# Mixers without GpSimd, latents with tokens on the partitions, and an output projection of plain fp32 products

## The chip, the core and the metric

The kernel runs on one core of a Trainium2 chip. The metric is the time of one execution on the device, in microseconds: the median of several runs. Of the core's engines the text speaks of TensorE (PE; PEld is its weight load), VectorE (DVE), ScalarE (ACT), GpSimd (POOL) and SyncE (SP), whose queue issues the weight loads.

## What is computed

The reference is a trunk of two layers over 256 tokens of width 1024 in fp32. One layer is

```python
x = x + 0.5 * swiglu(rms_norm(x, norm_ffn1[l]), ffn1_w13[l], ffn1_w2[l])
h = rms_norm(x, norm_mix[l])
proj = h @ w_in[l]
z, xbc, dt_raw, cq, ckv, kidx, widx, xl, gl = jnp.split(proj, offsets, axis=-1)
...
mixed = jnp.concatenate([y_ssd, y_att, y_lru], axis=-1)
x = x + mixed @ w_out[l]
x = x + 0.5 * swiglu(rms_norm(x, norm_ffn2[l]), ffn2_w13[l], ffn2_w2[l])
```

Between the two lines of `proj` and `mixed` stand three causal mixers. `ssd_mixer` (512 columns of `mixed`) passes `xbc` through a convolution of width 4 and a silu, forms a decay-weighted product over the tokens, multiplies by silu(z) and normalizes two groups of 256 columns per token: `rms_norm(yg, norm_g)`. `dsa_mixer` (256 columns) normalizes the latents `cq`, `ckv` and the index key `kidx` per token, selects 64 keys per query by an index score, and attends to them. `rglru_mixer` (256 columns) is a convolution, a linear recurrence over the tokens and a gate gelu(gl).

## The kernel before

Products of weights and activations are made of three fp32r products: each operand is split into a rounded part and a rest. `wsplit` does that for weights: ScalarE rounds (`whi`, L249), and another engine subtracts (`wlo`, L250). In the FFNs (`ffn`, L305) that other engine is DVE; in `mixers` (L367) the argument `eng` says which: DVE for the latents and the LRU input, GpSimd (G) for `xbc`, the gate `gl`, `z` and all of `w_out`. `mm3` (L239) and `mmt` (L253) issue the three products.

The mixers first project the latents (L399 to L416): `pair` and `block` put 128 columns of w_in on the partitions of PSUM and the 256 tokens along the row. The norms' sums of squares come from TensorE products with a column of ones (L423, L426), and the small columns are transposed back to tokens (L451). Then come the index score and the selection (`scores`, `select`), softmax and attention (`logits`, `softmax`, `weigh`), the decay matrices M0 and M1 (L643 on), the LRU (`lru`), four `xbc_pair`s with the convolution (`conv`, L668) and the silu, the gate (`lru_gate`), `z`, and the SSD products (L778, L779). At the end the group norm's factor is computed per token (L788 to L796), spread over the partitions by four transposes (L800), multiplied into y (L806), y is split (L808, L809), and `project` (L817) multiplies by w_out: first the LRU rows, then the attention rows, then the SSD rows, into four PSUM accumulators that stay open over all three. The last step adds them to the residual `X` (L832) and calls `finish`, which begins the next norm (`norm_block`, L272).

The program's order is not the source's: a scheduler places the instructions of every engine by its own simulated times, and each engine then runs its list in order. Weights come through a pool of four buffers (`wraw`) that the loads in SP's queue use in turn; the split parts have four buffers each. PSUM is in three pools: `gu` (three buffers), `acc` (two) and `sm` (three).

## Time and profile before

| | |
|---|---|
| median of 3 runs | 1076.36 us (1075.48 to 1077.21) |
| profiled execution | 1075.42 us, its span 1073.7 us |
| TensorE, DVE, ScalarE, GpSimd busy | 994.8, 699.1, 530.8, 139.9 us |
| mean granted clock of TensorE | 0.971 |
| read from HBM | 170.57 MB, 160 GB/s over the span |

The profile is one execution on the chip. Busy times are sums over the whole span and mix two kinds of stage, the FFNs and the mixers; a stretch has to be cut out to see what limits it. Matmuls are pipelined, so the duration of one is longer than the distance to the next one's start. Layer 0's mixers lie between about 211 and 358 us, layer 1's between about 734 and 881 us.

### The profile page before, as it was taken

How to read it: one execution, taken by the hardware profiler on the slowest of the kernel's cores; microseconds unless marked ns; L12 is line 12 of the kernel's file. 1: busy time of each engine (PE TensorE's matmuls, PEld its weight loads, DVE VectorE, ACT ScalarE, POOL GpSimd, SP SyncE). 2: the span in 40 equal slices, each digit the busy share in tenths (PEclk: the TensorE clock that was granted, in tenths of full speed). 3: DMA queues.
4: the chain of work that ended last, by engine and by line, in shares of the span. 5: the costliest groups of instructions: out<-in, count | busy, mean ns of one | idle time of the engine just before them, and what ended most of it. 6: DMA issues, size and time to landing. Idle time of an engine off the chain costs nothing.

```text
span 1073.7 us, 13352 instructions
## 1 busy us (share of the span) xinstructions
PE 994.8 (93%) x5003; PEld 832.7 (78%) x5003; DVE 699.1 (65%) x1221; ACT 530.8 (49%) x814; POOL 139.9 (13%) x91
## 2 busy tenths in 40 slices
PE   3999999999577999999999999999986779999998
PEld 2888888889475788888888888889876658888886
DVE  3666664579995766564566656455999666665643
ACT  4444544458442655454555544455765345454432
POOL 5100000034463000000000000002364310000000
PEclk9999999999788999999999999999997889999999
DMA  8855555553143366555656655566320435565560
GB/s 184 260 182 180 172 181 196 179 156 99 40 139 116 115 200 191 166 178 181 216 165 196 195 174 182 179 202 186 99 79 27 150 118 175 180 193 162 191 215 20
DMA packets 144833, 172.48 MB, mean 161 GB/s; under 512 B 4899, under 2 KB 116657, under 8 KB 144769
## 3 DMA queue, kind: packets, MB, share of 16 engines
q1 hardware_dynamic: 143840, 171.03, 49.8%
q0 software_dynamic: 896, 0.60, 1.0%
q8 instruction: 39, 0.64, 0.2%
q14 instruction: 26, 0.21, 0.1%
q10 hardware_dynamic: 32, 0.01, 0.0%
HBM read 170.57 MB, written 1.05 MB: 160 GB/s over the span
## 4 chain that ended last, share of the span: by engine, by line
PE 78%; DVE 18%; DMA 2%; ACT 1%; issue 1%; SPq 0%; ACTq 0%; DVEq 0%
PE gu L255 16%; PE gu L256 16%; PE gu L257 15%; PE acc L255 8%; PE acc L256 8%; PE acc L257 8%; DVE xbc L668 4%; PE sm L339 2%; DMA wraw<-in_ffn_w_dram 2%; DVE score L523 1%; DVE score L535 1%; DVE m L746 1%; DVE wlo L250 1%; PE gu L241 1%; DVE m L532 1%; PE gu L240 1%
## 5 line engine op out<-in xcount | busy, mean ns | idle before, releaser
L250 DVE TENSOR_TENSOR wlo<-wraw,whi 128x1024 fp32r<-128x1024 f32 x274 | 335.0, 1224 | 264.9 <-ACT whi L249 256.1
L249 ACT ACTIVATE whi<-wraw 128x1024 fp32r<-128x1024 f32 x322 | 337.7, 1052 | 314.0 <-PE gu L257 155.7
L255 PE MATMUL gu<-whi,xh 128*128 128x512 f32 x704 | 278.0, 398 | 11.3 <-ACT whi L249 9.6
L257 PE MATMUL gu<-whi,xl 128*128 128x512 f32 x704 | 276.6, 396 | 0.2
L256 PE MATMUL gu<-wlo,xh 128*128 128x512 f32 x704 | 274.7, 392 | 0.0
L250 POOL TENSOR_TENSOR wlo<-wraw,whi 128x1024 fp32r<-128x1024 f32 (+2 forms) x48 | 111.5, 2335 | 706.1 <-ACT whi L249 704.0
L255 PEld LDWEIGHTS gu<-whi,xh 128*128 128x128 f32 x704 | 132.9, 189 | 37.2 <-ACT whi L249 10.0
L257 PEld LDWEIGHTS gu<-whi,xl 128*128 128x128 f32 x704 | 132.6, 188 | 27.8 <-DVE xl L282 1.0
L256 PEld LDWEIGHTS gu<-wlo,xh 128*128 128x128 f32 x704 | 132.9, 189 | 27.3 <-DVE wlo L250 0.8
L257 PE MATMUL acc<-whi,hl 128*128 128x512 f32 x352 | 137.7, 391 | 0.0
L256 PE MATMUL acc<-wlo,hh 128*128 128x512 f32 x352 | 137.1, 389 | 0.0
L255 PE MATMUL acc<-whi,hh 128*128 128x512 f32 x352 | 135.7, 391 | 0.0
L240 PE MATMUL gu<-xh,whi 128*128 128x256 f32 (+1 forms) x320 | 94.4, 299 | 27.5 <-DVE cx L681 26.6
L241 PE MATMUL gu<-xl,whi 128*128 128x256 f32 (+1 forms) x320 | 95.1, 298 | 0.0
L242 PE MATMUL gu<-xh,wlo 128*128 128x256 f32 (+1 forms) x320 | 92.8, 291 | 0.0
L240 PEld LDWEIGHTS gu<-xh,whi 128*128 128x128 f32 (+1 forms) x320 | 61.8, 195 | 30.1 <-ACT th L674 26.9
L257 PEld LDWEIGHTS acc<-whi,hl 128*128 128x128 f32 x352 | 66.1, 188 | 13.6
L256 PEld LDWEIGHTS acc<-wlo,hh 128*128 128x128 f32 x352 | 66.1, 188 | 13.6
L255 PEld LDWEIGHTS acc<-whi,hh 128*128 128x128 f32 x352 | 66.1, 188 | 13.3
L334 ACT ACTIVATE th_s<-gu,rhalf 128x256 f32<-128x256 f32 x88 | 41.8, 475 | 69.0 <-PE gu L257 68.8
L241 PEld LDWEIGHTS gu<-xl,whi 128*128 128x128 f32 (+1 forms) x320 | 62.4, 195 | 2.2 <-issue 1.4
L242 PEld LDWEIGHTS gu<-xh,wlo 128*128 128x128 f32 (+1 forms) x320 | 62.4, 195 | 0.1
(350 smaller groups left out, 962.8 us busy)
## 6 DMA issues: line engine op xcount, KB each, us to landing
wraw<-in_ffn_w_dram SPq DMA_DIRECT2D x184, 512.0 KB, 4.8
wraw<-in_ffn_w_dram SPq DMA_DIRECT2D x40, 1024.0 KB, 5.0
...
wraw<-in_w_out_dram SPq DMA_DIRECT2D x8, 512.0 KB, 3.6
...
```

The source lines that it names most:

```text
L240: T.matmul(o, lh, rh, start=first, stop=False)
L241: T.matmul(o, lh, rl, start=False, stop=False)
L242: T.matmul(o, ll, rh, start=False, stop=last)
L249: S.activation(hi[sl], raw, AF.Copy)
L250: eng.tensor_sub(lo[sl], raw, hi[sl].bitcast(F32))
L255: T.matmul(o, xh, wh, start=first, stop=False)
L256: T.matmul(o, xh, wl, start=False, stop=False)
L257: T.matmul(o, xl, wh, start=False, stop=last)
L334: S.activation(th, ps[h][:, 0:256], AF.Tanh, scale=rh_[:, h:h + 1])
L339: T.transpose(pt[:, j * SEQ + h * P:j * SEQ + (h + 1) * P], hf[:, j * P:(j + 1) * P], ident)
L523: V.scalar_tensor_tensor(s2, rel[:, p_, :ns], wx[:, qb, hd:hd + 1], score, ALU.mult, ALU.add)
L668: V.scalar_tensor_tensor(dst[:, j, s:], xr[:, j, :SEQ - s], col(wname, l, (3 - s) * wm + m), dst[:, j, s:], ALU.mult, ALU.add)
```

## The change

- GpSimd has no more work in the mixers: all splits of w_in and the product of M0 go to DVE.
- The latents (460 columns, dt and the index key and weights among them) are projected with the tokens on the partitions, as in the FFN: three products of up to 460 columns for each of 8 rows of blocks and 2 halves of the tokens. ScalarE evicts them with the norm's factor per token as scale and sums their squares by rows; cq and ckv are transposed after that. The index key's rsqrt joins that of the other two.
- The output projection takes y, the attention and LRU outputs, and w_out as plain fp32, one product each, with no split. The attention and LRU rows are added to the residual first; the SSD rows are scaled by `ssd_norm` on ScalarE, and the group norm's factor is applied per token where the two halves of the groups are evicted into the residual: eight evictions in place of four.

```diff
-        ah, al = two("ah", 1, F32R), two("al", 1, F32R)
-        rh, rl = two("rh", 1, F32R), two("rl", 1, F32R)
+        ya_, yl_ = two("ya_", 1), two("yl_", 1)
...
-        raw0 = load_cols(C_DT, 264)
-        raw1 = load_cols(C_CKV, 196)
-        pcq = pair(raw0, 8, (V, V))
...
+        NS = C_XL - C_DT
+        O = 32 - (C_CQ - C_DT)
+        pS = [psg.tile([P, 512], F32, name="gu")[:, :NS] for _ in range(NH)]
+        for q in range(2):
+            raw = rp.tile([P, 4, 512], F32, name="wraw")
+            nc.sync.dma_start(raw[:, :, :NS], w_in[q * 512:(q + 1) * 512, C_DT:C_XL]
+                              .rearrange("(k p) c -> p k c", p=P))
+            ws = [wsplit([P, 2, 512], [((slice(None), slice(None), slice(0, NS)), raw[:, 2 * i:2 * i + 2, :NS])], V)
+                  for i in range(2)]
+            for h in range(NH):
+                hs = slice(h * P, (h + 1) * P)
+                for k in range(4):
+                    kk = 4 * q + k
+                    mmt(pS[h], n.h[kk][:, hs], n.l[kk][:, hs], ws[k // 2][0][:, k % 2, :NS],
+                        ws[k // 2][1][:, k % 2, :NS], kk == 0, kk == KD - 1)
+        cs = mp.tile([P, NH, 512], F32, name="cs", bufs=1)
+        for h in range(NH):
+            S.activation(cs[:, h, O:O + NS], pS[h], AF.Copy, scale=n.r[:, h:h + 1])
+        o_q, o_kv, o_ki, o_wi = (O + c - C_DT for c in (C_CQ, C_CKV, C_KI, C_WI))
+        lss = mp.tile([P, 3, NH], F32, name="lss", bufs=1)
+        for h in range(NH):
+            for i, (o, w) in enumerate(((o_q, 256), (o_kv, 128), (o_ki, 64))):
+                sq = mp.tile([P, 256], F32, name="lsq", bufs=1)
+                S.activation(sq[:, :w], cs[:, h, o:o + w], AF.Square, accum_out=lss[:, i, h:h + 1])
+        cq, ck = two("cq", 1), one("ck", 1)
+        ptq = att_ps()
+        ptk = att_ps()
         for h in range(NH):
             hs = slice(h * P, (h + 1) * P)
             for b in range(2):
-                T.matmul(pss[:, h:h + 1], sqc[:, b, hs], ones[:, 0:1], start=b == 0, stop=b == 1)
-        for h in range(NH):
-            hs = slice(h * P, (h + 1) * P)
-            T.matmul(pss[:, 2 + h:3 + h], sqc[:, 2, hs], ones[:, 0:1], start=True, stop=True)
-        r2 = mp.tile([P, NH], F32, name="r2", bufs=1)
-        V.tensor_mul(r2, n.r, n.r)
-        vc = mp.tile([P, 2, NH], F32, name="vc", bufs=1)
-        for i, dim in enumerate((256, 128)):
-            V.scalar_tensor_tensor(vc[:, i], pss[:, 2 * i:2 * i + 2], 1.0 / dim, r2, ALU.mult, ALU.mult)
-        V.tensor_scalar(vc, vc, RS, EPS * RS, ALU.mult, ALU.add)
-        sc = mp.tile([P, 2, NH], F32, name="sc", bufs=1)
+                T.transpose(ptq[:, b * SEQ + h * P:b * SEQ + (h + 1) * P], cs[:, h, o_q + b * P:o_q + (b + 1) * P], ident)
+            T.transpose(ptk[:, hs], cs[:, h, o_kv:o_kv + P], ident)
+        for b in range(2):
+            V.tensor_scalar(cq[:, b], ptq[:, b * SEQ:(b + 1) * SEQ], col("cq_norm", l, b), None, ALU.mult)
+        V.tensor_scalar(ck, ptk[:, :SEQ], col("ckv_norm", l, 0), None, ALU.mult)
+        vc = mp.tile([P, 3, NH], F32, name="vc", bufs=1)
+        for i, dim in enumerate((256, 128, 64)):
+            V.tensor_scalar(vc[:, i], lss[:, i], RS / dim, EPS * RS, ALU.mult, ALU.add)
+        sc = mp.tile([P, 3, NH], F32, name="sc", bufs=1)
         rsqrt_of(sc, vc, mp, "cr")
-        V.tensor_mul(sc, sc, n.r[:, None, :].to_broadcast([P, 2, NH]))
 
...
-        kss = mp.tile([P, NH], F32, name="kss", bufs=1)
-        ksq = mp.tile([P, NH, 64], F32, name="excl0", bufs=1)
-        S.activation(ksq, sm[:, :, 0:64], AF.Square)
-        V.tensor_reduce(kss, ksq, axis=AX.X, op=ALU.add)
-        kr = mp.tile([P, NH], F32, name="kr", bufs=1)
-        rsqrt(kr, kss, 1.0 / 64, mp, "kq")
         for h in range(NH):
-            V.scalar_tensor_tensor(TI[:, h, 4:6], sm[:, h, None, 0:64].to_broadcast([P, 2, 64]), kr[:, h:h + 1],
-                                   kig[:, l, None, :].to_broadcast([P, 2, 64]), ALU.mult, ALU.mult)
+            V.scalar_tensor_tensor(TI[:, h, 4:6], cs[:, h, None, o_ki:o_ki + 64].to_broadcast([P, 2, 64]),
+                                   sc[:, 2, h:h + 1], kig[:, l, None, :].to_broadcast([P, 2, 64]),
+                                   ALU.mult, ALU.mult)
...
-            S.copy(ah[:, :, qs], pt2)
-            V.tensor_sub(al[:, :, qs], pt2, ah[:, :, qs].bitcast(F32))
+            S.copy(ya_[:, :, qs], pt2)
...
-            ps = pair(load_cols(C_GL, 256), 0, (G, G))
+            ps = pair(load_cols(C_GL, 256), 0, (V, V))
...
-                V.scalar_tensor_tensor(gt[:, b], gt[:, b], 1.0, hx[:, b], ALU.add, ALU.mult)
-                S.copy(rh[:, b], gt[:, b])
-                V.tensor_sub(rl[:, b], gt[:, b], rh[:, b].bitcast(F32))
+                V.scalar_tensor_tensor(yl_[:, b], gt[:, b], 1.0, hx[:, b], ALU.add, ALU.mult)
...
-        xbc_pair(load_cols(C_XBC + 512, 256), 4, (G, G), picked)
-        xbc_pair(load_cols(C_XBC + 768, 256), 6, (G, G), picked)
+        xbc_pair(load_cols(C_XBC + 512, 256), 4, (V, V), picked)
+        xbc_pair(load_cols(C_XBC + 768, 256), 6, (V, V), picked)
...
-            G.tensor_mul(M0[g], M0[g], cb[:, None, :SEQ].to_broadcast([P, 4, SEQ]))
+            V.tensor_mul(M0[g], M0[g], cb[:, None, :SEQ].to_broadcast([P, 4, SEQ]))
             V.tensor_mul(M1[g], M1[g], cb[:, None, SEQ:].to_broadcast([P, 4, P]))
 
-        xbc_pair(load_cols(C_XBC, 256), 0, (G, G))
-        xbc_pair(load_cols(C_XBC + 256, 256), 2, (G, G))
+        xbc_pair(load_cols(C_XBC, 256), 0, (V, V))
+        xbc_pair(load_cols(C_XBC + 256, 256), 2, (V, V))
...
-            ps = pair(load_cols(C_Z + 256 * q, 256), 0, (G, G))
+            ps = pair(load_cols(C_Z + 256 * q, 256), 0, (V, V))
...
 
 
-        pss = small_ps()
+
+        w_out = A["w_out"][l]
+
+        def rows_of(k0, c):
+            raw = rp.tile([P, 4, 512], F32, name="wraw")
+            nc.sync.dma_start(raw, w_out[k0 * P:(k0 + 4) * P, c * 512:(c + 1) * 512]
+                              .rearrange("(k p) c -> p k c", p=P))
+            return raw
+
+        def project(ys, ws, h, c, scale=None):
+            acc = psg.tile([P, 512], F32, name="gu")
+            for t, (y, w) in enumerate(zip(ys, ws)):
+                T.matmul(acc, y[:, h * P:(h + 1) * P], w, start=t == 0, stop=t == len(ys) - 1)
+            xs = X[h][:, c * 512:(c + 1) * 512]
+            if scale is None:
+                V.tensor_add(xs, acc, xs)
+            else:
+                V.scalar_tensor_tensor(xs, acc, scale, xs, ALU.mult, ALU.add)
+
+        rest = [ya_[:, 0], ya_[:, 1], yl_[:, 0], yl_[:, 1]]
+        for c in range(2):
+            raw = rows_of(4, c)
+            for h in range(NH):
+                project(rest, [raw[:, t] for t in range(4)], h, c)
+
+        raws = [rows_of(0, c) for c in range(2)]
+        for c in range(2):
+            for t in range(4):
+                S.activation(raws[c][:, t], raws[c][:, t], AF.Copy, scale=col("ssd_norm", l, t))
+        yr = []
         for q in range(2):
+            pss = small_ps()
             sq = two("z", 2)
             S.activation(sq, yg[q], AF.Square)
             V.tensor_add(sq[:, 0], sq[:, 0], sq[:, 1])
             for h in range(NH):
-                T.matmul(pss[:, 2 * q + h:2 * q + h + 1], sq[:, 0, h * P:(h + 1) * P], ones[:, 0:1],
-                         start=True, stop=True)
-        yr = mp.tile([P, 2, NH], F32, name="yr", bufs=1)
-        yv = mp.tile([P, 4], F32, name="yv", bufs=1)
-        V.tensor_scalar(yv, pss[:, :4], RS / 256, 4.0 * EPS * RS, ALU.mult, ALU.add)
-        rsqrt_of(yr.rearrange("p q h -> p (q h)"), yv, mp, "yq")
-        pb = small_ps().rearrange("p (q t) -> p q t", q=2)
+                T.matmul(pss[:, h:h + 1], sq[:, 0, h * P:(h + 1) * P], ones[:, 0:1], start=True, stop=True)
+            yv = mp.tile([P, NH], F32, name="yv", bufs=2)
+            V.tensor_scalar(yv, pss[:, :NH], RS / 256, 4.0 * EPS * RS, ALU.mult, ALU.add)
+            r = mp.tile([P, NH], F32, name="yr", bufs=2)
+            rsqrt_of(r, yv, mp, "yq")
+            yr.append(r)
         for q in range(2):
             for h in range(NH):
-                bcast_rows(pb[:, q, h * P:(h + 1) * P], yr[:, q, h:h + 1])
-        sh = []
-        for q in range(2):
-            t = mp.tile([P, 2, 2, SEQ], F32R, name="m0", bufs=2)
-            for j in range(2):
-                b = 2 * q + j
-                V.scalar_tensor_tensor(yg[q][:, j], yg[q][:, j], col("ssd_norm", l, b), pb[:, q, :],
-                                       ALU.mult, ALU.mult)
-                S.copy(t[:, 0, j], yg[q][:, j])
-                V.tensor_sub(t[:, 1, j], yg[q][:, j], t[:, 0, j].bitcast(F32))
-                sh.append((t[:, 0, j], t[:, 1, j]))
-
-
-        accs = [[psa.tile([P, 512], F32, name="acc") for _ in range(NH)],
-                [psg.tile([P, 512], F32, name="gu") for _ in range(NH)]]
-        w_out = A["w_out"][l]
-
-        def project(k0, parts, eng, step):
-
-            nk = len(parts)
-            for c in range(2):
-                raw = rp.tile([P, nk, 512], F32, name="wraw")
-                nc.sync.dma_start(raw, w_out[k0 * P:(k0 + nk) * P, c * 512:(c + 1) * 512]
-                                  .rearrange("(k p) c -> p k c", p=P))
-                ws = [wsplit([P, 2, 512], [(slice(None), raw[:, i:i + 2])], eng) for i in range(0, nk, 2)]
-                for h in range(NH):
-                    hs = slice(h * P, (h + 1) * P)
-                    for t, (xh, xl) in enumerate(parts):
-                        mmt(accs[c][h], xh[:, hs], xl[:, hs], ws[t // 2][0][:, t % 2], ws[t // 2][1][:, t % 2],
-                            step == 0 and t == 0, step == 2 and t == nk - 1)
-                    if step == 2:
-                        xs = X[h][:, c * 512:(c + 1) * 512]
-                        V.tensor_add(xs, accs[c][h], xs)
+                for c in range(2):
+                    project([yg[q][:, 0], yg[q][:, 1]], [raws[c][:, 2 * q], raws[c][:, 2 * q + 1]], h, c,
+                            yr[q][:, h:h + 1])
+                    if q == 1:
                         finish(h, c)
-
-        project(6, [(rh[:, b], rl[:, b]) for b in range(2)], G, 0)
-        project(4, [(ah[:, b], al[:, b]) for b in range(2)], G, 1)
-        project(0, sh, G, 2)
 
 
     n = norm_begin()
```

How the scheduler orders it is read from the built programs, layer 0; "x2" is two rows alike.

DVE, from the convolution of the first two xbc pairs on (L668 before and L657 now are the convolution step, L250 the subtraction of a split, L585, L586 and L575, L576 softmax). Before:

```order
L668 SCALAR_TENSOR_TENSOR xbc<-cx,colT_104,xbc 128x255 x4
L713 SCALAR_TENSOR_TENSOR lb<-lt,lb 128x512
L668 SCALAR_TENSOR_TENSOR xbc<-cx,colT_104,xbc 128x254
L585 SCALAR_TENSOR_TENSOR prob<-ya,prob 128x1024
L668 SCALAR_TENSOR_TENSOR xbc<-cx,colT_104,xbc 128x254 x3
L715 SCALAR_TENSOR_TENSOR la_2413<-la,lb 128x256 x2
```

and now:

```order
L250 TENSOR_TENSOR wlo<-wraw,whi 128x1024
L710 TENSOR_TENSOR lx<-gu,nrb 128x512
L578 SCALAR_TENSOR_TENSOR mx<-mx,qr 128x4
L525 MATCH_REPLACE score_2056<-m_2051,score_2048 128x128
L700 SCALAR_TENSOR_TENSOR lt<-la_2341,lt 128x512
L531 SCALAR_TENSOR_TENSOR excl_2060<-score_2056,inv_208 128x128
L657 SCALAR_TENSOR_TENSOR xbc<-cx,colT_104,xbc 128x255 x4
L575 SCALAR_TENSOR_TENSOR rel<-excl_2060,rel 128x512
L657 SCALAR_TENSOR_TENSOR xbc<-cx,colT_104,xbc 128x254 x2
L250 TENSOR_TENSOR wlo<-wraw,whi 128x1024
L657 SCALAR_TENSOR_TENSOR xbc<-cx,colT_104,xbc 128x254 x2
```

The subtractions now stand in DVE's row among its other work; the second L250 here is the last one of w_in.

TensorE, from the transposes of xbc on (L755 before, L742 now; L255 to L257 are the three products of w_out before, L784 a plain one now; ya_ is the attention output, yl_ the LRU's). Before:

```order
L755 MATMUL acc<-ident,xbc 128x128 x8
L255 MATMUL gu<-whi,rh 128x512 x2
L616 MATMUL sm<-ident,ya 128x128 x2
L603 MATMUL sm<-ident,rel 128x128 x4
L256 MATMUL gu<-wlo,rh 128x512
L257 MATMUL gu<-whi,rl 128x512
```

and now:

```order
L606 MATMUL sm<-ident,ya 128x128 x2
L784 MATMUL gu<-wraw,ya__1784 128x512 x2
L784 MATMUL gu<-wraw,yl__1785 128x512 x2
L784 MATMUL gu<-wraw,ya__1784 128x512 x2
L784 MATMUL gu<-wraw,yl__1785 128x512 x2
L784 MATMUL gu<-wraw,ya__1784 128x512 x2
L742 MATMUL acc<-ident,xbc 128x128 x8
L784 MATMUL gu<-wraw,yl__1785 128x512 x2
```

Ten products of the output projection moved ahead of the transposes.

TensorE at the end of the mixers (L791 before and L808 now are the sums of squares for the group norm, L289 the spreading of the factor, la and la_2906 the two groups of y, L278 the transposes of the next norm). Before:

```order
L791 MATMUL sm<-ones,z 128x1 x2
L256 MATMUL gu<-wlo,ah 128x512
L257 MATMUL gu<-whi,al 128x512
L289 MATMUL sm<-ident,yr 128x128 x4
L255 MATMUL acc<-whi,m_3030 128x512
```

and now:

```order
L784 MATMUL gu<-wraw,la 128x512 x6
L808 MATMUL sm<-ones,z 128x1 x4
L784 MATMUL gu<-wraw,la 128x512 x2
L784 MATMUL gu<-wraw,la_2906 128x512 x6
L278 MATMUL sm<-ident,xr 128x128 x4
L784 MATMUL gu<-wraw,la_2906 128x512 x2
L278 MATMUL sm<-ident,xr 128x128 x8
```

Six products of the SSD rows moved ahead of the sums of squares; the spreading is gone.

## Rows read from the trace of the kernel before

**Rows 1.** The page: busy time of each engine, and the chain that ended last by engine.
```profile
PE 994.8 (93%) x5003; PEld 832.7 (78%) x5003; DVE 699.1 (65%) x1221; ACT 530.8 (49%) x814; POOL 139.9 (13%) x91
...
PE 78%; DVE 18%; DMA 2%; ACT 1%; issue 1%; SPq 0%; ACTq 0%; DVEq 0%
```

**Rows 2.** Busy us (x instructions) by stretch: PE, PEld, DVE, ACT, POOL; PEclk, DMA, GB/s.
```profile
228.80:321.55 92.75, 72.03 (x506) 66.41 (x505) 91.60 (x214) 55.46 (x112) 44.92 (x18) 0.87 0.28 92
751.50:844.00 92.50, 71.59 (x505) 66.02 (x505) 91.41 (x214) 55.48 (x112) 44.92 (x18) 0.89 0.28 92
```

**Rows 3.** Instructions in order of time, GpSimd and DVE: start us, us, engine, line, what.
```profile
229.57 2.38 POOL L250 TENSOR_TENSOR wlo<-wraw,whi 128x1024 fp32r<-128x1024 f32 x1 [1.08 <-DVE dtx L628]
...
229.62 2.35 DVE L174 SCALAR_TENSOR_TENSOR spa<-dtx 128x16 f32<-128x16 f32 x1
```

**Rows 4.** Groups of DVE by form, 210 to 360: busy us, mean ns, idle before.
```profile
L668 DVE SCALAR_TENSOR_TENSOR xbc<-cx,colT,xbc 128x254 f32<-128x254 f32 x8 | 11.5, 1464 | 0.0
L668 DVE SCALAR_TENSOR_TENSOR xbc<-cx,colT,xbc 128x255 f32<-128x255 f32 x8 | 7.8, 1014 | 0.0
L746 DVE TENSOR_TENSOR m<-m,cb 128x512 f32<-128x512 f32 x2 | 5.7, 2855 | 0.0
L668 DVE SCALAR_TENSOR_TENSOR xbc<-cx,colT,xbc 128x253 f32<-128x253 f32 x8 | 3.6, 468 | 0.0
L523 DVE SCALAR_TENSOR_TENSOR score<-rel,wx,score 128x256 f32<-128x256 f32 x3 | 3.0, 995 | 0.1
L713 DVE SCALAR_TENSOR_TENSOR lb<-lt,lb 128x512 f32<-128x512 f32 x1 | 2.8, 2823 | 0.0
L523 DVE SCALAR_TENSOR_TENSOR score<-rel,wx,score 128x128 f32<-128x128 f32 x3 | 2.8, 925 | 0.0
L725 DVE TENSOR_SCALAR lt<-lt 128x256 f32<-128x256 f32 x2 | 2.8, 1375 | 0.0
L668 DVE SCALAR_TENSOR_TENSOR lx<-cx,colT,lx 128x254 f32<-128x254 f32 x2 | 2.0, 982 | 0.0
L486 DVE TENSOR_TENSOR rp<-qk,rope 128x256 f32<-128x256 f32 x1 | 1.9, 1877 | 0.0
L541 DVE SCALAR_TENSOR_TENSOR ya<-score,inv 128x256 f32<-128x256 f32 x1 | 1.4, 1415 | 0.0
L711 DVE SCALAR_TENSOR_TENSOR lt<-la,lt 128x512 f32<-128x512 f32 x1 | 0.7, 674 | 0.0
```

**Rows 5.** The same view of the same stretch: DVE's subtractions.
```profile
L250 DVE TENSOR_TENSOR wlo<-wraw,whi 128x1024 fp32r<-128x1024 f32 x7 | 8.5, 1222 | 4.2 <-ACT whi L249 4.1
```

**Rows 6.** DVE in order of time, 321 to 322.
```profile
321.11 0.41 DVE L619 TENSOR_TENSOR al<-sm,ah 128x256 fp32r<-128x256 f32 x1
```

**Rows 7.** TensorE in order of time, 232 to 235.
```profile
232.39 1.88 PE L459 MATMUL sm<-wq,cq 128*128 128x512 f32 x4
234.11 1.02 PE L467 MATMUL sm<-wk,ck 128*128 128x512 f32 x2
```

**Rows 8.** TensorE in order of time, 312 to 316 and 359 to 360.
```profile
315.66 0.66 PE L755 MATMUL acc<-ident,xbc 128*128 128x128 f32 x2 [6.60 <-DVE xbc L675]
...
359.58 0.50 PE L255 MATMUL gu<-whi,xh 128*128 128x512 f32 x1 [0.79 <-ACT xh L281]
```

**Rows 9.** Busy us by stretch, columns as in rows 2.
```profile
318.00:320.00 2.00, 2.00 (x10) 1.70 (x9) 2.00 (x5) 1.10 (x4) 1.74 (x1) 0.50 0.00 2
320.00:322.00 2.00, 2.00 (x9) 1.65 (x8) 1.52 (x3) 0.46 (x1) 0.63 (x1) 0.88 0.11 17
```

**Rows 10.** Groups of TensorE by form, 210 to 360.
```profile
L778 PE MATMUL acc<-m,xdt 128*64 128x256 f32 x16 | 3.3, 398 | 0.0
```

**Rows 11.** DVE in order of time, 341.5 to 343.
```profile
341.83 0.16 DVE L166 SCALAR_TENSOR_TENSOR yqz<-yqt,yqy 128x4 f32<-128x4 f32 x1
342.02 0.16 DVE L162 TENSOR_TENSOR yqt<-yqz 128x4 f32<-128x4 f32 x1
```

**Rows 12.** The page: DMA issues, KB each, median us from issue to landing.
```profile
wraw<-in_ffn_w_dram SPq DMA_DIRECT2D x184, 512.0 KB, 4.8
```

More of the change, by code (lines that the diff above doesn't have):

```diff
@@ L396, in pair @@
             return ps
-        raw0 = load_cols(C_DT, 264)
-        raw1 = load_cols(C_CKV, 196)
-        pcq = pair(raw0, 8, (V, V))
-        cq = two("cq", 1)
-        for b in range(2):
-            V.tensor_scalar(cq[:, b], pcq[:, b], col("cq_norm", l, b), None, ALU.mult)
-        sqc = mp.tile([P, 3, SEQ], F32, name="sqc", bufs=1)
-        S.activation(sqc[:, 0:2], pcq, AF.Square)
-        pkv = psg.tile([P, 2, SEQ], F32, name="gu")
-        block(pkv[:, 0, :], wsplit([P, KD, P], [(slice(None), raw1[:, :, 0:P])], V))
```

21 lines of the change are left out of this document (3 added, 18 removed).

## The prediction

> **What bounds the kernel now.** I read the page's engine table and chain first, then busy time by stretch, then the mixers instruction by instruction. The page says that TensorE is busy for 93% of the span and that the chain which ends last runs 78% over PE and only 18% over DVE [rows 1]. That is an average over two kinds of stage, FFNs and mixers. In each mixer there is a stretch of 92.75 us (228.8 to 321.55 in layer 0, the same in layer 1) in which DVE is busy for 91.6 us while TensorE has work for 72 us [rows 2]: there DVE sets the time, and what the change is worth is read there and in the tail behind it.
>
> DVE is not busy with arithmetic alone. Where GpSimd runs, some DVE instructions end only when the GpSimd instruction ends: a 16-element-wide L174 that begins at 229.62 takes 2.35 us beside a GpSimd subtraction from 229.57 of 2.38 us [rows 3]. By form, the convolution step of 253 elements takes 468 ns, but that of 254 elements 1464 ns and that of 255 elements 1014 ns [rows 4]. One element does not cost that; the waits do. In the trace these are instructions with two operands in SBUF (and L725, which has one).
>
> **The change, part by part, for one layer.** Times are those of the profiled execution (1075.42 us, of which the span is 1073.7; the median of the runs is 0.94 us above it). I price layer 0 and count it twice, since the two stretches agree to 0.25 us [rows 2].
>
> *Waits that go.* I compare each slow form with the nearest undisturbed row: 468 ns for widths up to 256, 674 ns for 512 (L711) [rows 4]. Convolution steps: 8 x (1464 - 468) = 8.0 and 8 x (1014 - 468) = 4.4; L746: 2 x (2855 - 674) = 4.4; L523: 3 x 525 + 3 x 457 = 2.9; L713 2.1; L725 1.8; lx steps 1.0; L486 1.4; L541 0.9; L174 1.9. Sum 28.8 us, all inside the stretch. The instruction order of the change has no GpSimd row in the mixers, so all of it should go.
>
> *Work that comes to DVE.* Fourteen subtractions of 128x1024 move from GpSimd to DVE (eight for xbc, two for the gate, four for z). One takes 1222 ns on DVE [rows 5], and the following one starts a little before its end, so 1.15 each; one of them is done ahead of the stretch by the new order: 13 x 1.15 = 15.0. The two 128x1024 products of M0 have the same size and two SBUF operands: 2.3. Scaling cq and ck now falls into the stretch: 3 at about 0.4, 1.2.
>
> *Work that leaves DVE's stretch.* The low halves of the gate and of the attention output (three 256-wide at 0.41 [rows 6]) 1.2, two 512-wide xdt products, which the new order puts into the tail, 1.3, and the separate rsqrt of the index key with its reduction, a dozen narrow instructions at about 0.1 each (an estimate), 1.5. Together 4.0.
>
> The stretch becomes 92.75 - 28.8 + 15.0 + 2.3 + 1.2 - 4.0 = 78.45 us. DVE's queue is in order, and each subtraction now waits there for ScalarE's rounding with everything else behind it. The trace cannot show these waits, since GpSimd takes them now. Bounds: none, or all thirteen at the length of one subtraction (1.15), so 15.0. ScalarE is busy for only 55 of the 92.75 us [rows 2] and the order has other DVE work between the subtractions, so I take a value near the lower end, 1.4. The end of DVE's stretch (z's silu) moves from 321.1 (DVE is at L619 by then [rows 6]) to 228.8 + 78.45 + 1.4 = 308.65.
>
> *The latents.* 96 products of 256 columns become 48 of 460. By columns that is 24576 against 22080, with six transposes added and twelve sums by TensorE gone. TensorE gains about 1 us, the first DVE instruction may come 2 to 3 us earlier, but the q path has a transpose and an eviction more. I cost it at nothing, since DVE's queue behind it is full; the cover is the lru convolution and the subtractions.
>
> *The tail.* A plain fp32 product of 512 columns is two instructions: four such take 232.39 to 234.11, 0.43 each, so 0.86 a product [rows 7]. There are 32: 16 of the attention and LRU rows (the "rest"), 16 of the SSD rows. The new TensorE order puts ten rest products ahead of the xbc transposes, and they need the attention output. Behind its last DVE step (L602) stand M0, M1, two convolution steps, four silu steps, about 5.0 us, so it is ready at about 303.7, and transposed and copied at 304.9. TensorE idles before that, so the clock starts at its lower level: in before, idle time of 6.6 us ends at 315.66 [rows 8], and the granted clock still is 0.50, its lower level of 1.2 GHz, over 318 to 320 and at 0.88 over the next 2 us [rows 9]: some 4.4 us in which half the work is lost, 2.2. Then: ten products 8.6 + 2.2, at 315.7; eight transposes 1.1 (each at the mean of the stretch's 506 TensorE instructions, 72.03 us, so 0.142 [rows 2]), 316.8; six products 5.2, 322.0; the sixteen L778-type pairs 3.3 [rows 10], 325.3; six SSD products 5.2, 330.5; the sums of squares 0.5, 331.0. The order then holds TensorE: PSUM has three buffers for these, and the first can only be evicted once the group norm's factor is there. That is a chain of twelve DVE steps at 0.19 from start to start [rows 11], 2.3, and one eviction 0.8: 334.1. The remaining ten products 8.6 and four transposes 0.5, 343.2; eight transposes and the first xh 1.2: the FFN's first product at 344.4. In before it starts at 359.58 [rows 8]. From there both FFNs are bound by TensorE alike.
>
> What the tail loses, nothing hides; it begins 12.4 us earlier and is only some 2.8 us shorter in itself: no split of w_out on ScalarE and GpSimd, no rescaling of y, but dearer products. One queue is tight: DVE's row of FFN subtractions stands ahead of y, and their weights can only be fetched when the rest's buffer is read; a load takes 4.8 us from issue to landing [rows 12], which fits with less than 1 us to spare.
>
> Per layer 359.58 - 344.4 = 15.2; twice, 30.4. Profiled 1075.42 - 30.4 = 1045.0, so a median of **1046.0 us**.
>
> **Rivals.**
> *DVE waits for TensorE in its new queue.* With the splits on DVE, TensorE gets its weights later; its gaps spread over the stretch. A pair of blocks is 48 products, at the same 0.142 [rows 2] 6.8 us, and up to twice that at the lower clock; two pairs late by 6.8, less some 2 us of other DVE work each, cost 9 us a layer. For: z and the last xbc pair are scaled soon after the last split. Against: ten DVE instructions lie between. 1046 + 18 = 1064.
>
> *It packs better.* No waits (1.4), no cold start (2.2), the factor's chain hidden (3.1): 6.7 more a layer, 1032.6. For: DVE's first work may come earlier. Against: the chain stands in the order with nothing of TensorE's beside it.
>
> *The tail at the lower clock: slower.* All 32 products at 0.50 cost 27.5 us more, of which 2.2 is counted: 25.3 - 15.2 = 10.1 a layer above before, so 1076.4 + 20.2 = 1096.6. It decides from 20 of the 32 on (17.4 us at 0.86). For: the tail is where the granted clock falls in before [rows 9]. Against: in the same row it rises again while the products run. The Trainium skill (TensorE: Matmul & The Clock Gate, HAM oscillation) says that work in bursts with idle gaps falls back to the lower clock at every burst; by that rule alone the tail would be cold after the factor's wait too. The row shows the fall after idle and the rise within the same burst, so the trace agrees with the fall and not with a tail that stays cold.
>
> *The waits do not go.* If DVE's long forms were slow for another reason, the stretch would keep its 28.8: 28.8 - 15.2 = 13.6 a layer above before, 1076.4 + 27.2 = 1103.6. Against it: the ends coincide with GpSimd's [rows 3].
>
> **How the numbers follow.** Forecast 0.62, DVE waits for TensorE 0.17, better packing 0.13, cold tail 0.05, waits stay 0.03. Range 1031 to 1065: it takes in both faster neighbours and nearly all of the bounds of the waits (15.0 - 1.4 a layer would give 1073.2; the last of it I leave out as unlikely), and leaves out the two slow cases. About 0.2% (2 us) is what a measurement of this kernel can tell from no change. Faster 0.90, no change 0.03, slower 0.07.
>
> **What would show it.** Right: no GpSimd rows in the mixers; the 254- and 255-wide steps at 0.47 us like the 253-wide one; DVE's stretch near 80 us; TensorE idle for about 3 us before the seventh SSD product; the FFN's first product some 15 us earlier. Wrong: long two-operand DVE instructions that remain; DVE idle time before the scalings of z or xbc; a granted clock of 0.50 through most of the tail; the FFN starting with a gap for weights.

## The result, and the profile after

The changed kernel takes **1044.87 us** (median of four runs, 1043.16 to 1045.67) against 1075.92 us before (1074.78 to 1077.21): a ratio of 0.9709, 95% interval 0.9692 to 0.9726, 31.1 us less. The forecast was 1046.0 us, in a range of 1031 to 1065. The profiled execution took 1044.53 us, its span is 1042.8 us.

The page of the changed kernel, its engine table and its chain by engine, against [rows 1]:

```profile
PE 993.6 (95%) x4819; PEld 807.4 (77%) x4819; DVE 667.1 (64%) x1237; ACT 525.2 (50%) x822; POOL 18.3 (2%) x39
...
PE 86%; DVE 8%; DMA 4%; ACT 1%; issue 1%; SPq 0%; DVEq 0%; ACTq 0%
```

GpSimd keeps only the setup at the program's start, and DVE's share of the chain falls from 18% to 8%. Busy time by stretch (columns as in rows 2), from the first softplus step to the end of z's silu, in both layers:

```profile
226.90:307.20 80.30, 72.48 (x511) 64.50 (x510) 75.65 (x215) 59.13 (x124) 0.00 (x0) 0.94 0.28 93
...
732.50:813.70 81.20, 72.24 (x507) 64.20 (x506) 75.65 (x215) 59.06 (x123) 0.00 (x0) 0.94 0.28 91
```

DVE's stretch was 92.75 us, of which 91.60 busy [rows 2]; now it is 80.30, of which 75.65 busy, although thirteen of GpSimd's fourteen subtractions and both its products of 128x1024 now lie in it. Its groups by form, from 205 to 350 us (busy us, mean ns, idle before), and in order of time the small instruction that took 2.35 us [rows 3]:

```profile
L250 DVE TENSOR_TENSOR wlo<-wraw,whi 128x1024 fp32r<-128x1024 f32 x20 | 24.1, 1220 | 7.9 <-ACT whi L249 7.9
...
L657 DVE SCALAR_TENSOR_TENSOR xbc<-cx,colT,xbc 128x254 f32<-128x254 f32 x8 | 3.6, 477 | 0.0
L657 DVE SCALAR_TENSOR_TENSOR xbc<-cx,colT,xbc 128x253 f32<-128x253 f32 x8 | 3.6, 475 | 0.0
L657 DVE SCALAR_TENSOR_TENSOR xbc<-cx,colT,xbc 128x255 f32<-128x255 f32 x8 | 3.6, 480 | 0.4 <-ACT xbc L655 0.4
...
227.83 0.17 DVE L174 SCALAR_TENSOR_TENSOR spa<-dtx 128x16 f32<-128x16 f32 x1
```

The steps of 253, 254 and 255 elements cost the same now, where they had 468, 1464 and 1014 ns [rows 4]. The tail of layer 0 in order of time, TensorE:

```profile
302.44 2.07 PE L784 MATMUL gu<-wraw,ya__1784 128*128 128x512 f32 x2 [0.46 <-ACT ya__1784 L608]
...
322.83 5.42 PE L784 MATMUL gu<-wraw,la 128*128 128x512 f32 x12
328.08 0.50 PE L808 MATMUL sm<-ones,z 128*128 128x1 f32 x4
329.90 0.61 PE L808 MATMUL sm<-ones,z 128*128 128x1 f32 x4 [1.31 <-DVE z L806]
333.05 1.22 PE L784 MATMUL gu<-wraw,la 128*128 128x512 f32 x1 [2.55 <-DVE xr L789]
...
344.56 0.47 PE L255 MATMUL gu<-whi,xh 128*128 128x512 f32 x1
```

and what ScalarE and DVE did between the sixth and the seventh SSD product:

```profile
326.06 2.00 ACT L249 ACTIVATE whi<-wraw 128x1024 fp32r<-128x1024 f32 x2 [3.00 <-DMA wraw<-in_ffn_w_dram]
327.14 2.36 DVE L250 TENSOR_TENSOR wlo<-wraw,whi 128x1024 fp32r<-128x1024 f32 x2 [2.79 <-ACT whi L249]
327.97 0.61 ACT L805 ACTIVATE z<-la 128x512 f32<-128x512 f32 x1
...
329.42 0.42 DVE L806 TENSOR_TENSOR z<-z 128x256 f32<-128x256 f32 x1
...
329.76 0.15 DVE L810 TENSOR_SCALAR yv<-sm 128x2 f32<-128x2 f32 x1
...
332.25 2.06 DVE L789 SCALAR_TENSOR_TENSOR xr<-gu,yr,xr 128x512 f32<-128x512 f32 x3
```

The squares of the second half of y (L805) stand in ScalarE's queue behind two FFN splits that wait for their weights until 326.06; their sum (L806) stands in DVE's behind the low halves of the same weights. The eviction that frees the first PSUM buffer (L789) needs the factor of the first half alone; but the first step of that factor (L810) stands in DVE's queue behind all of these, and its sums on TensorE behind the six SSD products. So that factor is there at 332.1, and the seventh SSD product at 333.05, 4.9 us after TensorE had done the six that PSUM has room for. Busy time by stretch of the tail; the granted clock is the third number from the end:

```profile
302.00:306.00 4.00, 3.56 (x5) 1.70 (x6) 3.24 (x6) 1.68 (x4) 0.00 (x0) 0.55 0.00 0
306.00:322.00 16.00, 15.03 (x60) 7.47 (x59) 8.51 (x13) 2.47 (x3) 0.00 (x0) 1.00 0.25 73
328.00:333.00 5.00, 1.19 (x9) 0.93 (x7) 4.40 (x20) 0.58 (x2) 0.00 (x0) 0.99 0.46 138
333.00:336.00 3.00, 2.95 (x4) 1.40 (x5) 1.87 (x6) 0.00 (x0) 0.00 (x0) 0.50 0.36 127
336.00:344.00 8.00, 8.00 (x24) 3.72 (x24) 4.07 (x10) 2.79 (x8) 0.00 (x0) 0.98 0.11 29
```

TensorE starts the tail at its lower level, 1.2 GHz, rises, and after the wait for the factor is at 0.50 a second time.

Where the time came from, each position counted from the start of the last product of the FFN ahead. In layer 0 that start is at 210.80 us before and at 212.56 now; these 1.8 us are no part of the change, since two runs below with the changed kernel's order on TensorE have it at 210.61 and 211.60:

| us | before, layer 0 / 1 | after, layer 0 / 1 | less |
|---|---|---|---|
| FFN's last product to DVE's first softplus step (dtx) | 18.6 / 18.6 | 15.1 / 15.1 | 3.5 / 3.5 |
| from there to the end of z's silu | 91.8 / 91.8 | 79.6 / 80.6 | 12.2 / 11.2 |
| from there to the FFN's first product | 38.4 / 39.7 | 37.4 / 39.3 | 1.0 / 0.5 |

Of the runs below, one of four executions of one kernel (the factor early), the profiled one, was disturbed, 1310.66 us; it is left out of that run's time, and the kernel was run again for its trace.

### The profile page after: what moved, and what is told of

Same layout as the page of the kernel before. It is cut to its first block, busy times and chain, and to the rows that moved or that the text cites. A ratio compares the mean times of both kernels' runs of the same rounds, so it can differ in the third digit from the quotient of the medians.

```text
span 1042.8 us, 12881 instructions
## 1 busy us (share of the span) xinstructions
PE 993.6 (95%) x4819; PEld 807.4 (77%) x4819; DVE 667.1 (64%) x1237; ACT 525.2 (50%) x822; POOL 18.3 (2%) x39
## 4 chain that ended last, share of the span: by engine, by line
PE 86%; DVE 8%; DMA 4%; ACT 1%; issue 1%; SPq 0%; DVEq 0%; ACTq 0%
PE gu L255 16%; PE gu L256 16%; PE gu L257 16%; PE acc L255 8%; PE acc L256 8%; PE acc L257 8%; DMA wraw<-in_ffn_w_dram 4%; PE gu L784 4%; PE gu L240 2%; DVE wlo L250 2%; PE gu L241 2%; PE gu L242 2%; PE sm L339 2%; DVE xbc L657 1%; DVE score L525 1%; PE sm L278 1%
## 5 line engine op out<-in xcount | busy, mean ns | idle before, releaser
L250 DVE TENSOR_TENSOR wlo<-wraw,whi 128x1024 fp32r<-128x1024 f32 (+1 forms) x304 | 370.4, 1221 | 268.8 <-ACT whi L249 260.8
L249 ACT ACTIVATE whi<-wraw 128x1024 fp32r<-128x1024 f32 (+1 forms) x304 | 321.1, 1059 | 310.3 <-PE gu L257 158.5
L255 PE MATMUL gu<-whi,xh 128*128 128x512 f32 (+1 forms) x736 | 290.3, 397 | 10.0 <-ACT whi L249 10.0
L257 PE MATMUL gu<-whi,xl 128*128 128x512 f32 (+1 forms) x736 | 289.4, 396 | 0.0
L256 PE MATMUL gu<-wlo,xh 128*128 128x512 f32 (+1 forms) x736 | 287.1, 391 | 0.0
L255 PEld LDWEIGHTS gu<-whi,xh 128*128 128x128 f32 x736 | 139.1, 189 | 36.0 <-ACT whi L249 10.4
L257 PEld LDWEIGHTS gu<-whi,xl 128*128 128x128 f32 x736 | 138.8, 189 | 27.3
L257 PE MATMUL acc<-whi,hl 128*128 128x512 f32 x352 | 137.7, 391 | 0.0
L255 PE MATMUL acc<-whi,hh 128*128 128x512 f32 x352 | 135.7, 391 | 0.0
L240 PE MATMUL gu<-xh,whi 128*128 128x256 f32 x256 | 75.7, 296 | 4.7 <-DVE lx L710 4.7
L257 PEld LDWEIGHTS acc<-whi,hl 128*128 128x128 f32 x352 | 66.1, 188 | 13.6
L255 PEld LDWEIGHTS acc<-whi,hh 128*128 128x128 f32 x352 | 66.1, 188 | 13.4
L242 PE MATMUL gu<-xh,wlo 128*128 128x256 f32 x256 | 76.1, 297 | 0.0
L241 PE MATMUL gu<-xl,whi 128*128 128x256 f32 x256 | 75.2, 294 | 0.0
L240 PEld LDWEIGHTS gu<-xh,whi 128*128 128x128 f32 x256 | 50.4, 197 | 6.3 <-DVE lx L710 5.1
L242 PEld LDWEIGHTS gu<-xh,wlo 128*128 128x128 f32 x256 | 50.4, 197 | 1.7 <-issue 1.0
```

Source lines behind the costliest of these rows:

```text
L240: T.matmul(o, lh, rh, start=first, stop=False)
L241: T.matmul(o, lh, rl, start=False, stop=False)
L242: T.matmul(o, ll, rh, start=False, stop=last)
L249: S.activation(hi[sl], raw, AF.Copy)
L250: eng.tensor_sub(lo[sl], raw, hi[sl].bitcast(F32))
L255: T.matmul(o, xh, wh, start=first, stop=False)
```

## The experiments

Three theories were open: GpSimd's hold on DVE is what went (mine); the plain fp32 projection or the new latents carry the gain; the long DVE forms have another cause. "Hold" stands for the time by which a DVE instruction ends later beside one of GpSimd.

**The engine alone, done and undone.** In the kernel before, this part alone (and its reverse in the changed kernel):

```diff
-        xbc_pair(load_cols(C_XBC, 256), 0, (G, G))
+        xbc_pair(load_cols(C_XBC, 256), 0, (V, V))
...
-            G.tensor_mul(M0[g], M0[g], cb[:, None, :SEQ].to_broadcast([P, 4, SEQ]))
+            V.tensor_mul(M0[g], M0[g], cb[:, None, :SEQ].to_broadcast([P, 4, SEQ]))
```

> The kernel before with one part of the change alone: the low halves of w_in (xbc, gate, z) and the two products of M0 go from GpSimd to DVE; latents, output projection and its splits of w_out on GpSimd stay. Theory (GpSimd's instructions hold DVE's): of the 28.8 us of waits a layer most go, 14 subtractions (16.1) and M0 (2.3) come to DVE, some 1.4 of waits in its queue: 9.0 us a layer less, 18 in all, 1058 us; a little less if the splits of w_out that stay on GpSimd still hold DVE, so 1056 to 1064. The 254-wide convolution step near 0.48 us. Rival 1 (DVE's long forms have another cause): DVE only takes work, 18.4 us a layer more in a stretch that it bounds, 1113 us, the 254-wide step still 1.4 us. Rival 2 (the gain comes from the plain fp32 projection or the latents): no gain here, 1076 us or more.

Measured: 1058.68 us, ratio 0.9839 (0.9824 to 0.9853). Its DVE groups by form, and in order of time the one step of 255 elements that is long, with GpSimd's row beside it:

```profile
L668 DVE SCALAR_TENSOR_TENSOR xbc<-cx,colT,xbc 128x255 f32<-128x255 f32 x8 | 5.6, 744 | 0.0
...
L668 DVE SCALAR_TENSOR_TENSOR xbc<-cx,colT,xbc 128x253 f32<-128x253 f32 x8 | 3.5, 473 | 0.0
L668 DVE SCALAR_TENSOR_TENSOR xbc<-cx,colT,xbc 128x254 f32<-128x254 f32 x8 | 3.4, 471 | 0.0
...
291.98 3.20 POOL L250 TENSOR_TENSOR wlo<-wraw,whi 128x1024 fp32r<-128x1024 f32 x1 [1.47 <-ACT whi L249]
...
292.83 2.62 DVE L668 SCALAR_TENSOR_TENSOR xbc<-cx,colT,xbc 128x255 f32<-128x255 f32 x1
```

The 254-wide step is short at once. Of the eight 255-wide ones seven are short too (0.47 to 0.48 us); one takes 2.62 us, beside one of the splits of w_out that stay on GpSimd, and lifts the mean to 744 ns. More than half of the gain (17.2 of 31.1 us) comes from an edit that only gives DVE more work, so the rivals fall as causes of that part.

> The changed kernel with the same part alone undone: low halves of w_in for xbc, gate and z and the products of M0 on GpSimd again; token-major latents and the plain fp32 projection stay. Theory: the waits come back, 28.8 - 16.1 - 2.3 - 1.4 = 9 us a layer, 1063 us (1057 to 1070); GpSimd busy for some 43 us a layer; convolution steps of 254 and 255 elements over 0.9 us. Rival 1 (another cause for the long forms): DVE is only relieved, so the time stays at 1045 us or falls below. Rival 2 (projection or latents carry the gain): 1045 us, within 3.

Measured: 1048.89 us (0.9749, 0.9734 to 0.9764): only 4.0 us more than the changed kernel, well below what I expected. The stretch, from the FFN's last product to the end of z's silu, in this run and in the changed kernel:

```profile
211.31:312.71 101.40, 85.09 (x592) 77.85 (x591) 93.22 (x225) 67.65 (x144) 40.00 (x16) 0.92 0.33 108
```
```profile
212.56:307.19 94.63, 86.81 (x594) 77.65 (x593) 85.70 (x240) 68.65 (x145) 0.00 (x0) 0.95 0.36 115
```

Here DVE has 18.4 us of subtractions and products less to do and is busy for 7.5 us more; less the two xdt products that fall inside here (1.3), that is 24.6 us of hold for 40.0 us of GpSimd. So the waits did come back, and the stretch grew by 6.8 us. What I had not expected is that the tail got shorter by 2.7 us in layer 0 and 5.1 in layer 1: TensorE's order had changed with it.

```profile
317.63 1.98 PE L784 MATMUL gu<-wraw,ya__1784 128*128 128x512 f32 x4 [0.46 <-ACT ya__1784 L608]
...
332.27 12.29 PE L784 MATMUL gu<-wraw,la 128*128 128x512 f32 x28
...
347.35 0.48 PE L255 MATMUL gu<-whi,xh 128*128 128x512 f32 x1
```

All sixteen rest products stand here behind the SSD's own M times xdt, at full clock, and fourteen SSD products run on without a gap.

**The hold by itself.** Work on GpSimd that nobody needs, with every other engine's order as in the changed kernel (a scratch of the latents moves to another buffer to make room):

```diff
+        scr = mp.tile([P, 1024], F32, name="scr", bufs=1); G.memset(scr, 0.0)
+        G.tensor_copy(scr[:, 0:1], rb[:, 0:1]); [G.tensor_sub(scr, scr, scr) for _ in range(18)]
```

> The changed kernel with idle work for GpSimd at the start of each mixer's stretch: 18 subtractions of a 128x1024 scratch tile from itself, whose result nobody reads and no engine waits for; every other engine's order as in the changed kernel. Theory (a GpSimd instruction that reads SBUF holds DVE's instructions with two SBUF operands until it ends): about 18 x 2.4 = 43 us of GpSimd a layer; in the kernel before 44.9 us of GpSimd cost DVE 28.8, in the second run 40.0 us cost it some 26, so 20 to 28 us a layer here, 1085 to 1101 us. Rival (GpSimd is not what holds DVE; the long forms came with the weights' splits or the order): 1045 us, within 3.

Measured: 1094.04 us (1.0173, 1.0156 to 1.0190), 49.2 us more than the changed kernel, or 24.6 a layer (the profiled execution is the shortest of its five, 1089.12). GpSimd and DVE in order of time:

```profile
228.99 9.54 POOL L397 TENSOR_TENSOR scr<-scr 128x1024 f32<-128x1024 f32 x4
229.92 2.91 DVE L250 TENSOR_TENSOR wlo<-wraw,whi 128x1024 fp32r<-128x1024 f32 x1
232.75 1.85 DVE L435 TENSOR_SCALAR vc<-lss 128x2 f32<-128x2 f32 x1
```

Instruction by instruction against the changed kernel, 17 of DVE's are longer, by 26.2 us in all, nearly one for each of the 18 subtractions: a subtraction that alone takes 1.22 us takes 2.91, a two-element step 1.85 in place of 0.16, and the row behind that step begins 1.77 us after it where it began 0.07 after it. A product of 128x512 from PSUM that is not behind one of these keeps its 0.68 us.

> The same with 44 fills of the scratch tile with zeros (0.98 us each in the profile, 43 us a layer) in place of the 18 subtractions: GpSimd as long busy, but it reads nothing. The Trainium skill (SBUF - State Buffer, Who interferes with whom) says that only a GpSimd instruction that reads SBUF gets in the way of DVE's two-operand instructions. By a theory in which reading is what holds: 1045 us, within 3, convolution steps at 0.48 us. By one in which any GpSimd work beside DVE holds it: as much as in the run with the subtractions, 1085 us or more.

Measured: 1044.49 us (0.9707, 0.9693 to 0.9722), the changed kernel's time. In order of time:

```profile
229.23 7.04 POOL L397 MEMSET scr<- 128x1024 f32 x7
...
231.22 1.03 DVE L189 TENSOR_SCALAR spa<-dtx 128x16 f32<-128x16 f32 x1
...
231.89 1.22 DVE L250 TENSOR_TENSOR wlo<-wraw,whi 128x1024 fp32r<-128x1024 f32 x1
```

GpSimd is as long busy, and the two-operand subtraction keeps its 1.22 us. The theory by which reading holds stands, and the one by which any GpSimd work does falls. The Trainium skill's rule in that expectation agrees with this run, the two-operand rows at their own length beside the fills. Ten narrow one-operand TENSOR_SCALARs of layer 0 do end later here, by 0.15 to 0.87 us (the one of 16 elements with the end of a fill, 1.03 us), but the rows behind them are not held: here the next two begin 0.07 and 0.67 us after that one, in the changed kernel 0.08 and 0.68. The stretch ends 94.62 us behind the FFN's last product, and 94.64 in the changed kernel.

**The latents alone as before.** In the kernel before, GpSimd had two subtractions of the latents as well, those of their 76 odd columns (1.70 us in layer 0, ended at 213.73); here DVE has them.

```diff
-        NS = C_XL - C_DT
...
+        raw0 = load_cols(C_DT, 264)
+        raw1 = load_cols(C_CKV, 196)
+        pcq = pair(raw0, 8, (V, V))
...
```

> The changed kernel with the latents alone as before (96 products of 256 columns with the weights as the stationary side, sums of squares by products, the 76 odd columns with a transpose of their own; their low half on DVE, so GpSimd stays out). Theory: the latents are worth what DVE's first instruction comes earlier, 1.9 us a layer by the two traces, and the separate rsqrt of the index key, 1.5: 1045 to 1052 us. Rival (the latents carry the gain): 1060 us or more. The prediction's own step (nothing): 1045 us, within 2.

Measured: 1033.89 us (0.9605, 0.9589 to 0.9621), **11.0 us faster** than the changed kernel. Neither I nor the rival had that sign. The stretch from the FFN's last product to the end of z's silu, and TensorE's tail:

```profile
212.09:304.57 92.48, 85.61 (x637) 80.48 (x636) 85.89 (x256) 65.19 (x133) 0.00 (x0) 0.94 0.36 115
```
```profile
302.39 1.09 PE L751 MATMUL acc<-ident,xbc 128*128 128x128 f32 x4 [3.12 <-DVE xbc L673]
...
312.27 1.98 PE L793 MATMUL gu<-wraw,ya__1784 128*128 128x512 f32 x4
...
326.92 12.39 PE L793 MATMUL gu<-wraw,la 128*128 128x512 f32 x28
...
342.09 0.47 PE L255 MATMUL gu<-whi,xh 128*128 128x512 f32 x1
```

DVE has the same work in 2.2 us less, and the rest stands behind the SSD's products as in the run with the splits back on GpSimd. Two explanations remained: the new latents themselves, or the order that came with them (their attention output is there 88.7 us behind the FFN's last product instead of 95.8, so ten rest products got ahead of the xbc transposes).

> The changed kernel with one edge of order more on TensorE: the 16 products of the attention and LRU rows stand behind the SSD's own products (M times xdt), where they stood in the run with the old latents, in place of ten of them ahead of the xbc transposes. Theory (order): the new latents let the attention output come early, by which ten cold products got ahead of the transposes and delayed the group norm's factor; behind the SSD products they cover that factor's chain, so that the 4.9 us of idle TensorE before the seventh SSD product and the second start at the lower clock (2) go: 3 to 7 us a layer, 1031 to 1038 us. Rival (the new latents cost the 11 us by themselves): 1042 to 1046 us.

```diff
-                project(rest, [raw[:, t] for t in range(4)], h, c)
+                with tc.issue_after(pyi.ins):
+                    project(rest, [raw[:, t] for t in range(4)], h, c)
```

(`pyi` is the last product of M with xdt; the edge is one of order alone.) Measured: 1037.15 us (0.9645, 0.9628 to 0.9662), 7.7 less than the changed kernel, inside the theory's bounds:

```profile
313.25 1.98 PE L784 MATMUL gu<-wraw,ya__1784 128*128 128x512 f32 x4
...
327.89 12.39 PE L784 MATMUL gu<-wraw,la 128*128 128x512 f32 x28
```

The wait before the seventh SSD product is gone. By layer the FFN comes 1.7 and 5.6 us earlier; why layer 0 gains less was not followed (the transposes and the SSD's own products run at a granted clock of 0.50 there, from 304 to 312 us). So of the 11.0 us, 7.7 are the order. The 3.3 that are left go with the latents (by the traces 0.3 in layer 0, 1.8 in layer 1, and 0.7 of start); what makes them was not followed.

**The factor's wait, with the order kept:** the sums of squares behind the first and third SSD pair, the FFN's second pair of splits behind the factor, five PSUM buffers.

```diff
+                    for i in ((n.last,) if c == 1 else behind if c == 0 and q == 1 else ()):
+                        st.enter_context(tc.issue_after(i))
...
+            acc = mix_ps() if alt else psg.tile([P, 512], F32, name="gu")
...
+                    i = 4 * q + 2 * h + c
+                    with tc.issue_after(summed[i > 2]) if i > 0 else nullcontext():
```

> The changed kernel with its order of the rest kept (ten products ahead of the transposes), but the factor's wait attacked: the sums of squares stand behind the first and the third pair of SSD products on TensorE, the FFN's second pair of weight splits behind the factor on ScalarE and DVE, and the SSD products take five PSUM buffers (three and two) in place of three. Theory (the wait for the factor is what the tail lost): idle 4.9 and lower clock 2 go, 5 to 7 us a layer, 1031 to 1036 us. Rival (something else is late next: the xbc transposes, the FFN's weights): 1040 us or more.

Measured: 1031.74 us (0.9590, 0.9574 to 0.9606; the median of three). The same kernel a second time, for its trace:

> The kernel with the factor's wait attacked once more, for its trace. By the theory TensorE has no idle time over 1 us between the first SSD product and the last, no second run of products at 0.85 us an instruction, and the FFN's first product comes 125 to 127 us behind the last product of the FFN before (132.0 and 134.9 in the changed kernel); 1031 to 1036 us. Rival: the time came from elsewhere, and the seventh product still waits.

Measured: 1030.34 us (0.9576, 0.9562 to 0.9590). TensorE in order of time, and its stretches:

```profile
300.89 3.32 PE L786 MATMUL gu<-wraw,ya__1784 128*128 128x512 f32 x4 [0.46 <-ACT ya__1784 L610]
...
321.04 1.98 PE L786 MATMUL gu<-wraw,la 128*128 128x512 f32 x4
...
337.00 0.48 PE L255 MATMUL gu<-whi,xh 128*128 128x512 f32 x1
```
```profile
320.00:326.00 6.00, 6.00 (x29) 3.37 (x26) 4.73 (x18) 2.69 (x4) 0.00 (x0) 1.00 1.04 315
326.00:336.00 10.00, 10.00 (x30) 4.70 (x29) 8.24 (x21) 2.15 (x6) 0.00 (x0) 1.00 0.26 64
```

From the first SSD product to the last there is no idle time and no second fall of the clock; the FFN begins 126.0 and 127.1 us behind the last product of the one ahead (132.0 and 134.9 in the changed kernel). The wait for the factor cost the change 13 to 15 us (1044.87 less the two medians). What each of the three edits gives of that was not separated.

**By token halves:** the second half of the tokens first, three of four pieces ahead of the SSD's products.

```diff
+        for h in (1, 0):
+            for c in range(2):
+                with tc.issue_after(pyi.ins) if 2 * (1 - h) + c >= 3 else nullcontext():
```

> The run with the factor's wait attacked (1032.4 us), and the rest by token halves: the second half of the tokens first, whose attention output is there some 10 us before the other's (290.7 against 300.8 us in the changed kernel's trace) and which then waits for the gate's output at 297.1 alone; three of the four pieces stand ahead of the SSD's own products, the fourth behind them. Theory (from here on TensorE sets the tail): its first rest product comes at some 297.5 in place of 302.4, with up to 2 us of new idle behind it, so 3 to 4 us a layer less, 1024 to 1027 us. Rival (DVE's chain from z to the factor is next and sets the end): 1030 to 1033 us, the early products only moving the idle time.

Measured: **1021.26 us** (0.9477, 0.9458 to 0.9496), the fastest, and some 3 us below the range:

```profile
295.01 3.70 PE L786 MATMUL gu<-wraw,ya__1784 128*128 128x512 f32 x8 [0.64 <-ACT ya__1784 L610]
...
333.25 0.48 PE L255 MATMUL gu<-whi,xh 128*128 128x512 f32 x1
```
```profile
295.00:305.00 10.00, 8.81 (x30) 4.50 (x30) 10.00 (x20) 2.42 (x5) 0.00 (x0) 1.00 0.00 0
```

The first product comes at 295.0, close behind TensorE's other work, and is at full clock, so the cold start is gone as well: eight instructions take 3.70 us here, where in the run before the first four alone took 3.32. I had not counted that.

> The fastest run so far (token halves, factor early, 1021.3 us) with the latents alone as in the kernel before. With the rest behind the SSD products the old latents were 3.3 us faster than the new ones (1033.9 against 1037.2). Theory (the new latents are worth something only where TensorE takes the early attention output at once): here the first attention output comes some 10 us later again (12 us in the run with the old latents), so the rest's first product moves from 83 to some 93 us behind the FFN's last product, and the tail has some 5 us a layer less idle time to fill: 1027 to 1033 us. Rival (the old latents are faster anyhow): 1015 to 1019 us.

Measured: 1034.94 us (0.9625, 0.9609 to 0.9641), a little above the theory's range: the rest begins 93.3 us behind the FFN's last product in place of 83.2, and the FFN 129.4 in place of 121.5. The new latents cost 3.3 us in the one order and are worth 13.7 in the other.

**The projection alone as before**, with its splits on GpSimd (and the scratch of the latents moved, as above), and then the same with them on DVE:

```diff
+        project(6, [(rh[:, b], rl[:, b]) for b in range(2)], G, 0)
+        project(4, [(ah[:, b], al[:, b]) for b in range(2)], G, 1)
+        project(0, sh, G, 2)
```

> The changed kernel with the output projection alone as before: weights split (low halves on GpSimd), three products for each, the gated y scaled by the broadcast factor and split, attention and LRU outputs split. Theory: GpSimd is back only for the eight low halves of w_out, which hold DVE for a part of their 19 us, the low halves of the outputs are 1.2 us more on DVE, and the tail is some 0.7 us longer by the two traces: 1 to 6 us a layer, 1047 to 1057 us. Rival 2 (the plain fp32 projection carries the gain): 1070 us or more. A third possibility: the plain products cost more than the splits that they replace, since TensorE idles before the seventh and runs at its lower clock after it: below 1044 us.

> The run with the old output projection (1054.9 us), its eight low halves of w_out a layer moved from GpSimd to DVE. Theory (hold): in that run GpSimd was busy for 21.4 us a layer, at 26 us of hold for 40.0 us of GpSimd that is 13.9; eight subtractions at 1.15 come to DVE, 9.2: 4.7 a layer less, 1045 us, at most 1052 where TensorE and not DVE sets the end. Then the plain projection is worth little beyond keeping GpSimd out. Rival (the plain projection's gain is its own: fewer products, no splits, no scaling of y): 1055 us or more.

Measured: 1054.93 us (0.9803, 0.9785 to 0.9822) and 1043.85 us (0.9698, 0.9683 to 0.9712). GpSimd in the first, layer 0:

```profile
L250 POOL TENSOR_TENSOR wlo<-wraw,whi 128x1024 fp32r<-128x1024 f32 x8 | 21.0, 2633 | 278.2 <-ACT whi L249 278.2
```

Undoing the projection costs 10.1 us, but only because it brings GpSimd back: with the same three products and splits on DVE the time is that of the changed kernel, 1.0 us below it. As it stands, in its order, the plain fp32 projection is worth nothing beyond keeping GpSimd out. That is two things that cancel. In layer 0 of the run with the splits on DVE the stretch from the FFN's last product to the end of z's silu is 102.4 us, 7.8 longer than in the changed kernel, and the tail behind it 31.4, 6.0 shorter: what the plain projection takes off DVE, its wait for the factor gives back. With that wait out (the factor early, 1030.34) it is 13.5 us ahead of this run.

**The whole gain, step by step.** The kernels before and after and three of the runs differ by one part each: w_in's subtractions and M0 off GpSimd 17.2 us (1075.87 to 1058.68), the new latents 3.8 (to 1054.93), w_out's subtractions off GpSimd 11.1 (to 1043.85), the plain projection -1.0 (to 1044.87). So on this path 28.3 of the 31.1 us come from GpSimd. The sizes hold for this path alone, since each part moves the scheduler's order: taken out last, the latents came out as -11.0.

## Why the prediction was right, and where only the sum was

*Waits that go: right.* Forecast 28.8 us a layer; the second run shows 24.6 us for 40.0 us of GpSimd, the idle subtractions 26.2 for 39.7, so 0.6 to 0.7 us of DVE for each of GpSimd, and [rows 2, 4] give 28.8 for 44.92, 0.64. The engine alone came out at 1058.68 against 1058 forecast by the same terms. "The waits do not go" fell.

*Work to and from DVE, and in-order waits: right in their sum.* Forecast stretch 79.85 us, measured 80.30 in layer 0 and 81.20 in layer 1. In layer 0 two misses cancel: DVE is busy for 75.65 where the terms give 77.3, and idle for 4.65 in place of 1.15 before, so 3.5 us of new waits and not 1.4. "DVE waits for TensorE" would have wanted 9 us: its scalings of z have no idle time ahead, one of xbc has 0.6.

*The latents at nothing: the step that failed.* I wrote that DVE's queue behind them is full and hides them. DVE's first softplus step comes 3.5 us earlier than before (5.3 earlier than in the run with the old latents), but the end of z's silu is 2.2 us later than with the old latents on the same engines, since DVE idles for 8.9 us up to there instead of 6.6. And through the order that follows from their early attention output they cost 7.7 us more. By the runs they are not nothing: in the changed kernel's order they cost 11.0 us.

*The tail: right in its parts, its wait mis-sized.* The first rest product came at 302.4 (forecast 304.9), the last ends at 318.7 (322.0), the sixth SSD product at 328.3 (330.5): ahead of the forecast all along; the cold start cost 1.6 us (four instructions at 0.64 to 1.01 us from start to start in place of 0.43), priced at 2.2. Then 4.9 us passed from the sixth product to the seventh where I had 3.6 (330.5 to 334.1), because the factor's first steps stand behind FFN splits whose weights land late. I named that queue as tight by less than 1 us and priced it at nothing. After it four instructions took 0.69 to 1.01 us in place of 0.43: 1.7 us for a second start at the lower clock, which I had left out. By the last product the lead was gone: FFN at 344.56 against 344.4. The tail is 1.0 us shorter than before in layer 0, 0.5 in layer 1, not 2.8.

The Trainium skill (TensorE: Matmul & The Clock Gate, HAM oscillation) was weighed there as the rule by which the tail would be cold after the factor's wait too. The row of 333 to 336 at 0.50 agrees with that, and my sum should have had it. The rival, a tail that stays cold, falls: the row behind it has 0.98 while the products still run.

That the time came within 1.1 us is in part luck. By the table, over both layers, a start 7.0 us earlier than counted paid for a tail 4.1 us longer and a stretch 1.4 us longer than counted, and the 1.8 us at the program's start, which differ from execution to execution, took back what was left. "It packs better" was the right idea for another kernel: with the factor hidden and the cold start gone, 1021 us, below its 1032.6.
